# Out and down product with stationary weights, residual and result transposed, and squares of x moved up in a decoder block on one core

## The chip, the cores and the metric

One core of a Trainium2 chip runs the kernel. The metric is the device time in microseconds of one execution. A core has a matrix engine (TensorE, PE in the profile, with a row of its own, PEld, for loading the stationary operand), VectorE (DVE), ScalarE (ACT), GpSimd (POOL) and the queue engine SyncE (SP), which here issues the transfers of the weights. Each engine works through its own list in order; semaphores make one wait for another.

## The reference

A decoder block for 256 tokens of width 1024, all in float32:

```
n = rmsnorm(x, g1);  z = n @ w_in                       # 1024 x 7168, seven branches of 1024
y_conv = silu(layernorm(conv31(u * sigmoid(gate)))) @ w_conv_out
y_attn = attention(q, k, v with QK-norm and ALiBi, 8 heads) @ w_attn_out
merged = sigmoid(gc) * y_conv + sigmoid(ga) * y_attn
h   = x + merged @ w_out
out = h + (silu(m @ w_gate) * (m @ w_up)) @ w_down,     m = rmsnorm(h, g2)   # inner width 2816
```

Two parts matter here. The first RMS norm needs the sum of squares of each token of x over 1024 features; its factor is applied after the first products. The end of the block is the out product, the residual `h`, the second norm, gate and up product, and the down product with the residual added.

## The kernel before, in words

Every weight is float32 and is split into a high part (`whi`, a cast on ScalarE, line 154) and a low part (`wlo`, the difference, on VectorE or in some slots GpSimd, line 155); the activations are split in the same way. A product is three matmuls: high by high, low by high, high by low.

The work is a list of 146 slots, each with 512 KB of weights (128 partitions of 4 KB). The loop at the end of `hybrid_block` walks it. In each slot it first runs the closures in `pre`, then the first half of the slot's matmuls, issues the load and the split of weights for later slots (`AHEAD` = 6 slots for the split), runs `jobs`, then the second half, and then `post` and `late`. So the place of every instruction on every engine is set by the slot into which a closure was put. All engines follow the one written order.

There are two forms of a product. In `Chunk` slots the activations (transposed, features on partitions) are stationary and 512 columns of weights move; the result has tokens on partitions. `mm3` issues twelve matmuls of 512 columns a slot, six for each half of the tokens. In `Cols` slots a 128 x 128 tile of weights is stationary and the 256 tokens move; the result has output features on partitions. `mm_cols` issues 24 matmuls of 256 columns a slot. Before the change only gate-up (`gu`, 44 slots) is in the second form. In order, the slots are the convolution branch (16), q, k and v (24), the two gates (16), attention out (8), convolution out (`co`, 8), out product (`wo`, 8), `gu` (44) and down product (`dn`, 22).

The function `pair` makes the two tiles of a split activation; with `SHIFT` = 48 its data begin 48 floats, 192 bytes, into the tile. The pair `h`, which gate-up reads, has this shift; the pair `m`, which the out product reads, and the tiles `fh` and `fl`, which the down product reads, do not.

The start: x arrives transposed (`xt`); `split_x` makes its two parts, and `square` puts the squares of two k-tiles at a time on ScalarE, to be added on GpSimd (lines 713 and 715). `first_norm`, behind slot 4, sums them over the partitions with the matmul `ss` (line 727). VectorE and GpSimd make the factor `rstd` of it.

Around the out product: its result has tokens on partitions, is added to x in rows (`xs`, loaded for this, line 555), turned by sixteen transposes on PE (`htr`, line 565) and split from PSUM (`hh` on ScalarE, line 570, `hl` on VectorE, line 571). The sums of squares come from ScalarE's accumulator (line 577). The factor of the second norm is spread over the partitions by the product `rb` (line 607) as `row`; gate-up's gate half is multiplied by it, while its up half is not: that factor is applied with the residual when the down product is stored (`store`, line 651). The down product's last three slots are taken apart, so that the last store is small.

Of the kernel before, what the change touches and what calls it, by code (L numbers as in the profile page):

```python
# [82 lines left out]
GU_BANKS = ("cv0", "cv1", "mm", "mm", "mm", "mm")  # L83
GU_ORDER = halves_first(2 * KF, KD, len(GU_BANKS))


@with_exitstack
def hybrid_block(ctx: ExitStack, tc: tile.TileContext, x, xT, par, w_in, w_co, w_ao, w_o, w_gu, w_dn, out):
# [40 lines left out]
    def stream_dma(upto):  # L129
        while at["dma"] < min(upto, len(slots)):  # L130
            i = at["dma"]
            c, g = slots[i]
            raw[i] = wp.tile([P, *shape_of(i)], F32, tag="raw", bufs=RAW_BUFS, name=f"raw{i}")
            for part in parts(i):
                if i == 0:
                    load_x(part.start, part.stop)
                (nc.sync if i or part.start else nc.scalar).dma_start(raw[i][:, part, :], c.w[g][:, part, :])
                between(i, part)
            at["dma"] += 1
# [25 lines left out]
    def mm3(c, i, g, t, acc=None, cols=slice(0, CW), first=0, last=None):  # L165

        xh, xl = c.lhs()
        acc = c.acc[t] if acc is None else acc
        last = c.nk - 1 if last is None else last
        tok = slice(t * P, (t + 1) * P)  # L170
        for j in range(G):
            k = g * G + j
            nc.tensor.matmul(acc, xh[:, k, tok], hi[i][:, j, cols], start=(k == first), stop=False)  # L173
            nc.tensor.matmul(acc, xl[:, k, tok], hi[i][:, j, cols], start=False, stop=False)  # L174
            nc.tensor.matmul(acc, xh[:, k, tok], lo[i][:, j, cols], start=False, stop=(k == last))  # L175
# [3 lines left out]
    def mm_cols(c, i, g, units, slot):  # L179
        xh, xl = c.rhs()  # L180
        for u in units:
            n, k = c.order[g * U + u]
            c.seen[n] += 1
            first, last = c.seen[n] == 1, c.seen[n] == c.nk
            if first:
                tag = GU_BANKS[banks["n"] % len(GU_BANKS)]
# [11 lines left out]
    xt = ea.tile([P, XG + KD * S], F32, tag="vs", name="xt")  # L198
    xs = cst.tile([P, T, D], F32, name="xs")
# [318 lines left out]
    def merge_done(b):  # L518
        cols = slice(b * CW, (b + 1) * CW)

        def done(slot, acc):
# [6 lines left out]
            def turn():  # L528
                if not mT:
                    mT[0] = pair("m")  # L530
# [16 lines left out]
    s2 = sm.tile([P, 128], F32, bufs=1, name="s2")[:, : 2 * T].rearrange("p (t b) -> p t b", b=2)  # L547

    def out_done(b):
        cols = slice(b * CW, (b + 1) * CW)  # L550

        def done(slot, acc):
# [36 lines left out]
            late[slot + 2].append(squares)  # L589
        return done  # L590


    ff, gates, second = {}, {}, {}
# [5 lines left out]
    def spread2():  # L599
# [11 lines left out]
    def ffn_done(slot, n, acc):  # L611

# [25 lines left out]
        if not up:  # L638
            st["at"] = at_ = max(slot + 1, gu_slot + 5)
# [8 lines left out]
    def store(b, t, acc, cols=slice(0, CW)):  # L648
        to = slice(b * CW + cols.start, b * CW + cols.stop)
        o = sm.tile([P, cols.stop - cols.start], F32, tag="u", name=f"o{b}{t}{cols.start}")  # L650
        nc.vector.scalar_tensor_tensor(o, acc, rstd2[:, t : t + 1], xs[:, t, to], op0=ALU.mult, op1=ALU.add)
        nc.sync.dma_start(out[t * P : (t + 1) * P, to], o)

    def down_done(b):
        def done(slot, acc):
            if b == 0:
                late[slot + 1].append(lambda: [store(b, t, acc[t]) for t in range(T)])
        return done
# [17 lines left out]
    for b in range(2):  # L676
        add(Chunk(f"dn{b}", w_dn[b], lambda: ff[0], KF, down_done(b)))
# [39 lines left out]
    for i in range(6):  # L717
# [4 lines left out]
        if i >= 2:  # L722
            square(i - 2)
# [11 lines left out]
    late[16].append(lambda: nc.scalar.dma_start(xs, x.rearrange("(t p) d -> p t d", p=P)))  # L735
# [3 lines left out]
    n = len(slots)  # L739
    tail = 3  # L740
    split_k = KF - tail * G
    for slot, (c, g) in enumerate(slots):
# [7 lines left out]
        if rows and slot < n - tail:  # L750
            mm3(c, slot, g, 0)
# [6 lines left out]
        elif slot < n - tail:  # L758
            mm3(c, slot, g, 1, last=split_k - 1 if c is slots[-1][0] else None)
            if slot == n - tail - 1:  # L760
                end = xs[:, 1, D - CW :]
                nc.vector.scalar_tensor_tensor(end, c.acc[1], rstd2[:, 1:2], end, op0=ALU.mult, op1=ALU.add)
            for job in post.pop(slot, ()):
                job()
        elif slot == n - 1:
            for i in range(tail):
                mm3(c, n - tail + i, g - tail + 1 + i, 0)
            store(1, 0, c.acc[0])
            for part in range(2):
                cols = slice(part * CW // 2, (part + 1) * CW // 2)  # L770
                end = bank(f"end{part}", CW // 2)
                for i in range(tail):
                    mm3(c, n - tail + i, g - tail + 1 + i, 1, end, cols, first=split_k)
                store(1, 1, end, cols)
# [63 lines left out]
```

## Time and profile before

| | us |
|---|---|
| median of 3 timed runs | 440.75 (440.18 to 441.38) |
| the profiled execution, its own time | 441.83 |
| its span, first to last instruction | 440.0 |
| PE busy in the span | 433.4 (98%) |
| VectorE, ScalarE, GpSimd busy | 316.7, 247.8, 90.1 |

The busy share of PE is that of matmuls whose ends are modelled, and a matmul that waits for its operands can look busy. What PE does between two matmuls is read from their starts. The chain of waits gives 93% of the span to PE. The transfers move 182 GB/s on average and come several slots ahead of use after the first microseconds. The granted clock of TensorE is 1.00 nearly everywhere, with one dip in the first tenth of the span.

### The profile page before, as it was taken

How to read it: one execution, taken by the hardware profiler on the slowest of the kernel's cores; microseconds unless marked ns; L12 is line 12 of the kernel's file. 1: busy time of each engine (PE TensorE's matmuls, PEld its weight loads, DVE VectorE, ACT ScalarE, POOL GpSimd, SP SyncE). 2: the span in 40 equal slices, each digit the busy share in tenths (PEclk: the TensorE clock that was granted, in tenths of full speed). 3: DMA queues.
4: the chain of work that ended last, by engine and by line, in shares of the span. 5: the costliest groups of instructions: out<-in, count | busy, mean ns of one | idle time of the engine just before them, and what ended most of it. 6: DMA issues, size and time to landing. Idle time of an engine off the chain costs nothing.

```text
span 440.0 us, 6863 instructions
## 1 busy us (share of the span) xinstructions
PE 433.4 (98%) x2514; PEld 378.1 (86%) x2514; DVE 316.7 (72%) x558; ACT 247.8 (56%) x451; POOL 90.1 (20%) x74
## 2 busy tenths in 40 slices
PE   8899999999999999999999999999999999999996
PEld 4678888888888888888888899999999999888886
DVE  4989998998889799967759368666666666744501
ACT  6844466779998776558525267554444444533300
POOL 1615575643655424200000000000000000000000
PEclk9989999999999999999999999999999999999999
DMA  8975573556435435554745545555555555766101
GB/s 276 346 263 209 193 292 119 182 192 203 141 136 192 144 112 176 192 191 144 242 160 176 194 137 194 190 194 192 193 191 192 192 195 192 251 223 198 44 0 49
DMA packets 23346, 80.30 MB, mean 182 GB/s; under 512 B 2576, under 2 KB 3216, under 8 KB 23312
## 3 DMA queue, kind: packets, MB, share of 16 engines
q1 hardware_dynamic: 22752, 78.40, 52.7%
q10 hardware_dynamic: 560, 1.46, 0.9%
q8 instruction: 20, 0.33, 0.3%
q14 instruction: 14, 0.11, 0.1%
HBM read 78.80 MB, written 1.05 MB: 181 GB/s over the span
## 4 chain that ended last, share of the span: by engine, by line
PE 93%; ACT 2%; POOL 2%; DMA 1%; DVE 1%; SPq 0%; issue 0%
PE gu L191 9%; PE gu L192 9%; PE gu L190 9%; PE dn L174 4%; PE dn L175 4%; PE dn L173 4%; PE g L175 3%; PE g L173 3%; PE g L174 3%; PE conv L173 2%; PE conv L175 2%; PE conv L174 2%; PE k L175 2%; PE k L173 2%; PE v L175 2%; PE q L173 2%
## 5 line engine op out<-in xcount | busy, mean ns | idle before, releaser
L155 DVE TENSOR_TENSOR wlo<-raw,whi 128x1024 fp32r<-128x1024 f32 (+1 forms) x125 | 155.0, 1258 | 25.9 <-ACT whi L154 25.0
L154 ACT CAST whi<-raw 128x1024 fp32r<-128x1024 f32 (+1 forms) x149 | 150.4, 1033 | 36.7 <-PE dn L174 19.9
L190 PE MATMUL gu<-hh,whi 128*128 128x256 f32 x352 | 97.8, 278 | 0.0
L191 PE MATMUL gu<-hl,whi 128*128 128x256 f32 x352 | 97.6, 277 | 0.1
L192 PE MATMUL gu<-hh,wlo 128*128 128x256 f32 x352 | 97.4, 277 | 0.0
L273 DVE SCALAR_TENSOR_TENSOR cacc<-cv,prm,cacc 128x256 f32<-128x256 f32 x240 | 97.1, 474 | 0.2
L155 POOL TENSOR_TENSOR wlo<-raw,whi 128x1024 fp32r<-128x1024 f32 x24 | 60.7, 2536 | 50.4 <-ACT whi L154 45.5
L191 PEld LDWEIGHTS gu<-hl,whi 128*128 128x128 f32 x352 | 66.1, 188 | 0.4 <-DVE hl L571 0.3
L190 PEld LDWEIGHTS gu<-hh,whi 128*128 128x128 f32 x352 | 66.1, 188 | 0.3 <-ACT hh L570 0.2
L192 PEld LDWEIGHTS gu<-hh,wlo 128*128 128x128 f32 x352 | 66.2, 188 | 0.0
L175 PE MATMUL dn<-wlo,fh 128*128 128x512 f32 x82 | 31.9, 389 | 0.0
L174 PE MATMUL dn<-whi,fl 128*128 128x512 f32 x82 | 31.9, 389 | 0.0
L173 PE MATMUL dn<-whi,fh 128*128 128x512 f32 x82 | 31.9, 389 | 0.0
L173 PE MATMUL conv<-whi,xgh 128*128 128x512 f32 x64 | 26.3, 412 | 0.4 <-ACT whi L154 0.4
L173 PE MATMUL g<-whi,xgh 128*128 128x512 f32 x64 | 26.4, 412 | 0.0
L626 DVE TENSOR_TENSOR f<-gu,fs 128x256 f32<-128x256 f32 x22 | 9.2, 424 | 23.0 <-PE gu L192 23.0
L175 PE MATMUL conv<-wlo,xgh 128*128 128x512 f32 x64 | 25.7, 402 | 0.0
L174 PE MATMUL conv<-whi,xgl 128*128 128x512 f32 x64 | 25.7, 402 | 0.0
L175 PE MATMUL g<-wlo,xgh 128*128 128x512 f32 x64 | 25.1, 393 | 0.0
L174 PE MATMUL g<-whi,xgl 128*128 128x512 f32 x64 | 25.0, 390 | 0.0
L633 ACT CAST fh<-f 128x256 fp32r<-128x256 f32 x22 | 8.8, 406 | 26.8 <-DVE f L626 26.7
L622 ACT ACTIVATE fs<-fg 128x256 f32<-128x256 f32 x22 | 9.1, 417 | 25.4 <-DVE fg L618 25.4
(163 smaller groups left out, 747.6 us busy)
## 6 DMA issues: line engine op xcount, KB each, us to landing
raw<-in_w_in SPq DMA_DIRECT2D x53, 512.0 KB, 4.1
raw<-in_w_gu SPq DMA_DIRECT2D x44, 512.0 KB, 3.3
raw<-in_w_dn SPq DMA_DIRECT2D x22, 512.0 KB, 4.0
raw<-in_w_ao SPq DMA_DIRECT2D x8, 512.0 KB, 3.3
raw<-in_w_co SPq DMA_DIRECT2D x8, 512.0 KB, 3.3
raw<-in_w_o SPq DMA_DIRECT2D x8, 512.0 KB, 4.7
raw<-in_w_in SPq DMA_DIRECT2D x5, 256.0 KB, 5.6
xs<-in_x ACTq DMA_DIRECT2D x1, 1024.0 KB, 4.8
```

The costliest lines, as they stand in the source:

```text
L154: nc.scalar.copy(hi[i][:, part, :], r[:, part, :])
L155: eng.tensor_sub(lo[i][:, part, :], r[:, part, :], hi[i][:, part, :].bitcast(F32))
L173: nc.tensor.matmul(acc, xh[:, k, tok], hi[i][:, j, cols], start=(k == first), stop=False)
L174: nc.tensor.matmul(acc, xl[:, k, tok], hi[i][:, j, cols], start=False, stop=False)
L175: nc.tensor.matmul(acc, xh[:, k, tok], lo[i][:, j, cols], start=False, stop=(k == last))
L190: nc.tensor.matmul(acc, hi[i][:, u, :], xh[:, k, :], start=first, stop=False)
L191: nc.tensor.matmul(acc, hi[i][:, u, :], xl[:, k, :], start=False, stop=False)
L192: nc.tensor.matmul(acc, lo[i][:, u, :], xh[:, k, :], start=False, stop=last)
L273: nc.vector.scalar_tensor_tensor(cacc[j], src, w, cacc[j], op0=ALU.mult, op1=ALU.add)
L622: nc.scalar.activation(st["s"], st["g"], AF.Silu)
L626: nc.vector.tensor_mul(st["f"], acc, st["s"])
L633: nc.scalar.copy(ff[0][0][:, j, :], st["f"])
```

## The change

The out product and the down product become `Cols` slots, with weights stationary and 256 tokens moving. Their weights are laid out in 128 x 128 tiles on the host, in orders `O_ORDER` and `DN_ORDER` that take the first columns by halves of k. `xt` stays to the end; the residual is added to it in transposed form as each 128 output features are done, and the result is stored as 1024 x 256 and transposed on the host. The load of x in rows is gone, as are the transposes `htr`. The sum of squares for the second norm is now the squares of the transposed `h` (ScalarE), added up on GpSimd, and a small product `ss2` on PE. The up half of gate-up is multiplied by `row` as well. The pairs of `m` and `f` get the 192 bytes. At the start, the first two k-tiles of x are one transfer, all on SP's queue; the first two slots take their matmuls k-tile by k-tile for both halves of the tokens; and the squares of x stand one step earlier.

```diff
-GU_BANKS = ("cv0", "cv1", "mm", "mm", "mm", "mm")
-GU_ORDER = halves_first(2 * KF, KD, len(GU_BANKS))
+BANKS = ("cv0", "cv1", "mm", "mm", "mm", "mm")
+O_ORDER = halves_first(KD, KD, KD // 2)
+GU_ORDER = halves_first(2 * KF, KD, len(BANKS))
+DN_ORDER = halves_first(KD, KF, 2)
...
-                if i == 0:
-                    load_x(part.start, part.stop)
-                (nc.sync if i or part.start else nc.scalar).dma_start(raw[i][:, part, :], c.w[g][:, part, :])
+                if i == 0 and part.start == 0:
+                    load_x(0, 2)
+                nc.sync.dma_start(raw[i][:, part, :], c.w[g][:, part, :])
...
-    xt = ea.tile([P, XG + KD * S], F32, tag="vs", name="xt")
-    xs = cst.tile([P, T, D], F32, name="xs")
+    xt = cst.tile([P, XG + KD * S], F32, name="xt")
...
-                    mT[0] = pair("m")
+                    mT[0] = pair("m", SHIFT)
...
-            def evac():
-                for t in range(T):
-                    nc.vector.tensor_add(xs[:, t, cols], xs[:, t, cols], acc[t])
-
-            def turn():
-                if not hT:
-                    hT[0] = pair("h", SHIFT)
-                hh, hl = hT[0]
-                for k2 in (4 * b, 4 * b + 2):
-                    tr = bank(f"htr{k2}", 2, S)
-                    for j in range(2):
-                        for t in range(T):
-                            nc.tensor.transpose(tr[:, j, t * P : (t + 1) * P],
-                                                xs[:, t, (k2 + j) * P : (k2 + j + 1) * P], ident)
-                    for j in range(2):
-                        k = k2 + j
-                        g = prm[:, C_G2 + k : C_G2 + k + 1]
-                        nc.scalar.activation(hh[:, k, :], tr[:, j, :], AF.Copy, scale=g)
-                        nc.vector.scalar_tensor_tensor(hl[:, k, :], tr[:, j, :], g, hh[:, k, :].bitcast(F32),
-                                                       op0=ALU.mult, op1=ALU.subtract)
-
-            def squares():
-                for t in range(T):
-                    junk = sm.tile([P, CW], F32, tag="u", name="junk2")
-                    nc.scalar.activation(junk, xs[:, t, cols], AF.Square, accum_out=s2[:, t, b : b + 1])
-                if not b:
-                    second["ones"] = sm.tile([P, P], F32, tag="junk", bufs=1, name="allone")
-                    nc.gpsimd.memset(second["ones"], 1.0)
-                else:
-                    nc.vector.tensor_add(rstd2, s2[:, :, 0], s2[:, :, 1])
-                    rsqrt_mean(rstd2, rstd2, D, T)
-                    spread2()
-                    jobs[slot + 5].append(row2)
-
-            pre[slot + 1].append(evac)
-            jobs[slot + 2].append(turn)
-            late[slot + 2].append(squares)
...
+    def out_done(slot, j, acc):
+        h = xk(j, j + 1)[:, 0, :]
+        g = prm[:, C_G2 + j : C_G2 + j + 1]
+
+        def residual():
+            if not hT:
+                hT[0] = pair("h", SHIFT)
+            nc.vector.tensor_add(h, h, acc)
+
+        def high():
+            nc.scalar.activation(hT[0][0][:, j, :], h, AF.Copy, scale=g)
+
+        def low():
+            nc.vector.scalar_tensor_tensor(hT[0][1][:, j, :], h, g, hT[0][0][:, j, :].bitcast(F32),
+                                           op0=ALU.mult, op1=ALU.subtract)
+
+        def square2():
+            sq = free(f"hsq{j}")
+            nc.scalar.activation(sq, h, AF.Square)
+            if "sum" in second:
+                nc.gpsimd.tensor_add(second["sum"], second["sum"], sq)
+            else:
+                second["sum"] = free("hsum", "kT")
+                second["ones"] = sm.tile([P, P], F32, tag="junk", bufs=1, name="allone")
+                nc.gpsimd.memset(second["ones"], 1.0)
+                nc.gpsimd.tensor_copy(second["sum"], sq)
+
+        pre[slot + 1].append(residual)
+        late[slot + 1].append(high)
+        late[slot + 1].append(square2)
+        pre[slot + 2].append(low)
+        if j == KD - 1:
+            jobs[slot + 2].append(root2)
+            jobs[slot + 4].append(row2)
...
+    def root2():
+        ss = bank("ss2", T)
+        for t in range(T):
+            nc.tensor.matmul(ss[:, t : t + 1], second["sum"][:, t * P : (t + 1) * P], second["ones"][:, :1],
+                             start=True, stop=True)
+        nc.vector.tensor_scalar(rstd2, ss, 1.0 / D, EPS, op0=ALU.mult, op1=ALU.add)
+        nc.gpsimd.tensor_tensor(rstd2, rstd2, mhalf[:, :T], op=ALU.pow)
...
-            nc.vector.tensor_mul(st["f"], acc, st["s"])
+            nc.vector.tensor_mul(st["f"], acc, second["row"])
+            nc.vector.tensor_mul(st["f"], st["f"], st["s"])
...
-                ff[0] = (late_pool.tile([P, KF, S], F32R, name="fh"), late_pool.tile([P, KF, S], F32R, name="fl"))
+                ff[0] = tuple(
+                    late_pool.tile([P, KF * S + P], F32R, name="f" + x)[:, SHIFT : SHIFT + KF * S]
+                    .rearrange("p (k s) -> p k s", s=S) for x in "hl"
+                )
...
+    def down_done(slot, j, acc):
+        def evac():
+            o = sm.tile([P, S], F32, tag="u", name=f"o{j}")
+            nc.vector.tensor_add(o, acc, xk(j, j + 1)[:, 0, :])
+            nc.sync.dma_start(out[j * P : (j + 1) * P, :], o)
+
+        if j == KD - 1:
+            ends.append(evac)
+        else:
+            late[slot + 1].append(evac)
...
-    add(*(Chunk(f"wo{b}", w_o[b], lambda: mT[0], KD, out_done(b)) for b in range(2)))
+    add(Cols("wo", w_o, lambda: mT[0], KD, O_ORDER, out_done))
...
-        add(Chunk(f"dn{b}", w_dn[b], lambda: ff[0], KF, down_done(b)))
+    add(Cols("dn", w_dn, lambda: ff[0], KF, DN_ORDER, down_done))
...
-        if i >= 2:
-            square(i - 2)
+        if 1 <= i < 5:
+            square(i - 1)
...
-    late[16].append(lambda: nc.scalar.dma_start(xs, x.rearrange("(t p) d -> p t d", p=P)))
...
+        if slot < 2:
+            for j in range(G):
+                for t in range(T):
+                    mm3(c, slot, g, t, pieces=(j,))
+        elif rows:
```

On ScalarE at the start of the program, the casts of the weights (`whi`, the third to the sixth slot's) stand with the squares of x (`sq`, `xsq`) and its split (`xgh`). Before:

```order
L698 ACTIVATE xgh<-xt 128x256 x2
L154 CAST whi_170<-raw_134 128x512 x2
L698 ACTIVATE xgh<-xt 128x256 x2
L709 ACTIVATE sq_145<-xt 128x512
L154 CAST whi_181<-raw_138 128x1024
L712 ACTIVATE xsq_185<-xt 128x512
L154 CAST whi_188<-raw_140 128x1024
L712 ACTIVATE xsq_192<-xt 128x512
```

And after the change:

```order
L709 ACTIVATE sq_142<-xt 128x512
L156 CAST whi_168<-raw_131 128x512 x2
L698 ACTIVATE xgh<-xt 128x256 x2
L712 ACTIVATE xsq_178<-xt 128x512
L156 CAST whi_181<-raw_135 128x1024
L712 ACTIVATE xsq_185<-xt 128x512
L156 CAST whi_188<-raw_137 128x1024
L712 ACTIVATE xsq_192<-xt 128x512
L156 CAST whi_196<-raw_139 128x1024
```

All four squares stand ahead of the cast that they followed, the first of them ahead of the third slot's two casts.

On PE the out product (`wo`) is followed by gate-up (`gu`). Before, the transposes `htr` of the residual's second half stand among gate-up's matmuls in its second slot:

```order
L190 MATMUL gu_2621<-hh,whi_2495 128x256
L191 MATMUL gu_2621<-hl,whi_2495 128x256
L192 MATMUL gu_2621<-hh,wlo_2496 128x256
L565 MATMUL htr_2640<-ident,xs 128x128 x4
L565 MATMUL htr_2649<-ident,xs 128x128 x4
L190 MATMUL gu_2658<-hh,whi_2495 128x256
L191 MATMUL gu_2658<-hl,whi_2495 128x256
```

After the change `ss2`, the second sum of squares, stands in the same slot:

```order
L192 MATMUL gu_2740<-hl,whi_2565 128x256
L193 MATMUL gu_2740<-hh,wlo_2566 128x256
L597 MATMUL ss_2759<-allone,hsum 128x1 x2
L191 MATMUL gu_2767<-hh,whi_2565 128x256
L192 MATMUL gu_2767<-hl,whi_2565 128x256
L193 MATMUL gu_2767<-hh,wlo_2566 128x256
```

The eight transposes are gone here, as are the eight in the out product's last slot, and two short matmuls that read GpSimd's sum `hsum` have come in.

On VectorE in the out product, the low parts of the weights (`wlo`) stand with the residual. Before, the residual was two operations for each half of the columns, and `hl` came from the transposes:

```order
L155 TENSOR_TENSOR wlo_2514<-raw_2405,whi_2513 128x1024
L555 TENSOR_TENSOR xs<-xs,wo_0_2397 128x512
L555 TENSOR_TENSOR xs<-xs,wo_1_2398 128x512
L155 TENSOR_TENSOR wlo_2534<-raw_2423,whi_2533 128x1024
L155 TENSOR_TENSOR wlo_2552<-raw_2457,whi_2551 128x1024
L571 SCALAR_TENSOR_TENSOR hl<-htr_2557,prm,hh 128x256 x2
L571 SCALAR_TENSOR_TENSOR hl<-htr_2566,prm,hh 128x256 x2
L555 TENSOR_TENSOR xs<-xs,wo_0_2449 128x512
L555 TENSOR_TENSOR xs<-xs,wo_1_2450 128x512
```

After the change, each 128 features have an addition to `xt` and, a slot later, a low part `hl`:

```order
L559 TENSOR_TENSOR xt<-xt,wo_2393 128x256
L559 TENSOR_TENSOR xt<-xt,wo_2412 128x256
L157 TENSOR_TENSOR wlo_2520<-raw_2341,whi_2519 128x1024
L565 SCALAR_TENSOR_TENSOR hl<-xt,prm,hh 128x256 x2
L559 TENSOR_TENSOR xt<-xt,wo_2425 128x256
L559 TENSOR_TENSOR xt<-xt,wo_2458 128x256
L157 TENSOR_TENSOR wlo_2566<-raw_2359,whi_2565 128x1024
L565 SCALAR_TENSOR_TENSOR hl<-xt,prm,hh 128x256 x2
L559 TENSOR_TENSOR xt<-xt,wo_2550 128x256
L157 TENSOR_TENSOR wlo_2608<-raw_2406,whi_2607 128x1024
L565 SCALAR_TENSOR_TENSOR hl<-xt,prm,hh 128x256
```

The residual's operations are smaller and are spread over the out product's slots, one or two before each low part of the weights.

## Rows read from the trace of the kernel before

**Rows 1.** The page, busy time of PE and its share of the span.

```profile
PE 433.4 (98%) x2514; PEld 378.1 (86%) x2514; DVE 316.7 (72%) x558; ACT 247.8 (56%) x451; POOL 90.1 (20%) x74
```

**Rows 2.** Timeline of PE, 19.8 to 27.5: start, length, engine, line, operation, wait.

```profile
20.11 0.39 PE L175 MATMUL conv<-wlo,xgh 128*128 128x512 f32 x1
22.31 0.60 PE L727 MATMUL ss<-ones,sq 128*128 128x1 f32 x4 [1.80 <-POOL sq L715]
...
23.32 0.57 PE L175 MATMUL conv<-wlo,xgh 128*128 128x512 f32 x1
...
26.97 0.39 PE L175 MATMUL conv<-wlo,xgh 128*128 128x512 f32 x1
```

**Rows 3.** Busy time by stretch: PE, PEld, DVE, ACT, POOL, then granted clock, DMA.

```profile
23.40:26.70 3.30, 3.30 (x10) 2.53 (x9) 2.27 (x3) 0.21 (x1) 0.86 (x2) 0.50 0.86 290
...
254.20:256.30 2.10, 1.96 (x13) 1.52 (x12) 1.56 (x4) 1.52 (x5) 0.00 (x0) 1.00 0.21 86
...
269.80:370.00 100.20, 100.20 (x886) 100.20 (x885) 65.47 (x98) 52.07 (x79) 0.00 (x0) 1.00 0.59 200
```

**Rows 4.** Chain of waits: start, length, what.

```profile
259.39 0.87 PE htr L565 x8
```

**Rows 5.** Timeline of PE, gate-up up to the product rb.

```profile
254.65 0.38 PE L191 MATMUL gu<-hl,whi 128*128 128x256 f32 x1
...
256.28 0.28 PE L192 MATMUL gu<-hh,wlo 128*128 128x256 f32 x1
...
257.10 0.28 PE L190 MATMUL gu<-hh,whi 128*128 128x256 f32 x1
...
268.58 0.59 PE L607 MATMUL rb<-diag,allone 128*128 128x256 f32 x2
```

**Rows 6.** Timeline of PE, steady stretches of down product and gate-up.

```profile
409.81 0.39 PE L173 MATMUL dn<-whi,fh 128*128 128x512 f32 x1
...
411.17 0.39 PE L173 MATMUL dn<-whi,fh 128*128 128x512 f32 x1
...
289.78 0.28 PE L190 MATMUL gu<-hh,whi 128*128 128x256 f32 x1
...
290.46 0.28 PE L190 MATMUL gu<-hh,whi 128*128 128x256 f32 x1
```

**Rows 7.** Chain of waits, the last pieces of the down product.

```profile
435.05 0.12 PE end L174
```

**Rows 8.** Timeline of PE, ACT and DVE in the out product.

```profile
235.33 1.08 ACT L538 ACTIVATE mh<-mtr 128x512 fp32r<-128x512 f32 x2 [3.38 <-PE mtr L536]
...
235.49 0.48 PE L173 MATMUL wo<-whi,mh 128*128 128x512 f32 x1
...
235.96 0.69 DVE L539 SCALAR_TENSOR_TENSOR ml<-mtr,mh 128x512 fp32r<-128x512 f32 x1
```

**Rows 9.** Groups of instructions: shape, count, busy time, mean ns, idle before.

```profile
L618 DVE TENSOR_TENSOR fg<-gu,row 128x256 f32<-128x256 f32 x22 | 9.2, 423 | 15.2 <-PE gu L192 14.8 <-ACT row L609 0.4
```

**Rows 10.** Timeline of POOL at the start.

```profile
14.30 6.28 POOL L713 TENSOR_TENSOR sq<-sq,xsq 128x512 f32<-128x512 f32 x3 [11.81 <-ACT xsq L712]
20.66 1.59 POOL L715 TENSOR_TENSOR sq<-sq 128x256 f32<-128x256 f32 x1
```

**Rows 11.** Timeline of DVE at the start.

```profile
13.73 1.23 DVE L155 TENSOR_TENSOR wlo<-raw,whi 128x1024 fp32r<-128x1024 f32 x1 [0.72 <-ACT whi L154]
15.19 10.41 DVE L155 TENSOR_TENSOR wlo<-raw,whi 128x1024 fp32r<-128x1024 f32 x6 [0.24 <-ACT whi L154]
```

**Rows 12.** Timeline of ACT at the start.

```profile
12.13 0.62 ACT L709 ACTIVATE sq<-xt 128x512 f32<-128x512 f32 x1
12.66 1.04 ACT L154 CAST whi<-raw 128x1024 fp32r<-128x1024 f32 x1
13.60 0.63 ACT L712 ACTIVATE xsq<-xt 128x512 f32<-128x512 f32 x1
```

**Rows 13.** Timeline of PE, third matmul of slot 3.

```profile
15.35 0.39 PE L175 MATMUL conv<-wlo,xgh 128*128 128x512 f32 x1
```

More of the change, by code (lines that the diff above doesn't have):

```diff
@@ L80, in halves_first, with hybrid_block @@
     return out + [(c, k) for c in range(first, cols) for k in range(nk)]
-GU_BANKS = ("cv0", "cv1", "mm", "mm", "mm", "mm")
-GU_ORDER = halves_first(2 * KF, KD, len(GU_BANKS))
+BANKS = ("cv0", "cv1", "mm", "mm", "mm", "mm")
+O_ORDER = halves_first(KD, KD, KD // 2)
+GU_ORDER = halves_first(2 * KF, KD, len(BANKS))
+DN_ORDER = halves_first(KD, KF, 2)
 @with_exitstack
-def hybrid_block(ctx: ExitStack, tc: tile.TileContext, x, xT, par, w_in, w_co, w_ao, w_o, w_gu, w_dn, out):
+def hybrid_block(ctx: ExitStack, tc: tile.TileContext, xT, par, w_in, w_co, w_ao, w_o, w_gu, w_dn, out):
     nc = tc.nc
@@ L163, in pair, with mm3 @@
         )
-    def mm3(c, i, g, t, acc=None, cols=slice(0, CW), first=0, last=None):
+    def mm3(c, i, g, t, pieces=range(G)):
         xh, xl = c.lhs()
-        acc = c.acc[t] if acc is None else acc
-        last = c.nk - 1 if last is None else last
+        acc = c.acc[t]
         tok = slice(t * P, (t + 1) * P)
-        for j in range(G):
+        for j in pieces:
             k = g * G + j
-            nc.tensor.matmul(acc, xh[:, k, tok], hi[i][:, j, cols], start=(k == first), stop=False)
-            nc.tensor.matmul(acc, xl[:, k, tok], hi[i][:, j, cols], start=False, stop=False)
-            nc.tensor.matmul(acc, xh[:, k, tok], lo[i][:, j, cols], start=False, stop=(k == last))
+            nc.tensor.matmul(acc, xh[:, k, tok], hi[i][:, j, :], start=(k == 0), stop=False)
+            nc.tensor.matmul(acc, xl[:, k, tok], hi[i][:, j, :], start=False, stop=False)
+            nc.tensor.matmul(acc, xh[:, k, tok], lo[i][:, j, :], start=False, stop=(k == c.nk - 1))
     banks = {"n": 0}
@@ L185, in mm_cols @@
             if first:
-                tag = GU_BANKS[banks["n"] % len(GU_BANKS)]
+                tag = BANKS[banks["n"] % len(BANKS)]
                 banks["n"] += 1
@@ L197, in hybrid_block, with xk @@
     prm = cst.tile([P, N_PAR], F32, name="prm")
-    xt = ea.tile([P, XG + KD * S], F32, tag="vs", name="xt")
-    xs = cst.tile([P, T, D], F32, name="xs")
+    xt = cst.tile([P, XG + KD * S], F32, name="xt")
+    def xk(k0, k1):
+        return xt[:, XG + k0 * S : XG + k1 * S].rearrange("p (k s) -> p k s", s=S)
     warm = cst.tile([P, P], BF16, name="warm")
@@ L593, in hybrid_block @@
-    ff, gates, second = {}, {}, {}
+    second = {}
+    def out_done(slot, j, acc):
[27 more added lines that the diff above has]
+            jobs[slot + 4].append(row2)
@@ L595, in free @@
+    ff, gates = {}, {}
     def free(name, tag="qT"):
         return sm.tile([P, S], F32, tag=tag, bufs=4, name=name)
-    def spread2():
+    def root2():
[5 more added lines that the diff above has]
+        nc.gpsimd.tensor_tensor(rstd2, rstd2, mhalf[:, :T], op=ALU.pow)
@@ L638, in ffn_done @@
         if not up:
-            st["at"] = at_ = max(slot + 1, gu_slot + 5)
+            st["at"] = at_ = max(slot + 1, gu_slot + 4)
             pre[at_].append(scaled)
@@ L646, in ffn_done @@
             pre[at_ + 1].append(low)
[L648 to L658, printed above, removed]
+    ends = []
+    def down_done(slot, j, acc):
[7 more added lines that the diff above has]
+            late[slot + 1].append(evac)
     for p in range(KD // 2):
@@ L672, in hybrid_block @@
     add(*(Chunk(f"co{b}", w_co[b], lambda: yT[0], KD, merge_done(b)) for b in range(2)))
-    add(*(Chunk(f"wo{b}", w_o[b], lambda: mT[0], KD, out_done(b)) for b in range(2)))
+    add(Cols("wo", w_o, lambda: mT[0], KD, O_ORDER, out_done))
     gu_slot = len(slots)
     add(Cols("gu", w_gu, lambda: hT[0], KD, GU_ORDER, ffn_done))
-    for b in range(2):
-        add(Chunk(f"dn{b}", w_dn[b], lambda: ff[0], KF, down_done(b)))
+    add(Cols("dn", w_dn, lambda: ff[0], KF, DN_ORDER, down_done))
     xg[0] = pair("xg")
-    def xk(k0, k1):
-        return xt[:, XG + k0 * S : XG + k1 * S].rearrange("p (k s) -> p k s", s=S)
     def load_x(k0, k1):
@@ L734, in hybrid_block @@
     late[0].append(lambda: nc.scalar.dma_start(prm, par))
-    late[16].append(lambda: nc.scalar.dma_start(xs, x.rearrange("(t p) d -> p t d", p=P)))
     late[TABLE_SLOT].append(lambda: load_table(AF.Silu))
-    n = len(slots)
-    tail = 3
-    split_k = KF - tail * G
     for slot, (c, g) in enumerate(slots):
@@ L749, in hybrid_block @@
             c.acc = [ps.tile([P, CW], F32, tag="mm", bufs=4, name=f"{c.name}_{t}") for t in range(T)]
-        if rows and slot < n - tail:
+        if slot < 2:
[3 more added lines that the diff above has]
+        elif rows:
             mm3(c, slot, g, 0)
@@ L757, in hybrid_block @@
             mm_cols(c, slot, g, range(U // 2, U), slot)
[L758 to L774, printed above, removed]
+        elif slot >= 2:
+            mm3(c, slot, g, 1)
+        for job in post.pop(slot, ()):
+            job()
         load["pe"] += SLOT + pe_side.get(slot, 0.0)
@@ L781, in hybrid_block @@
             c.done(slot, c.acc)
+    for job in ends:
+        job()
     assert not (pre or jobs or post or late)
@@ L815 @@
     arrays = {
-        "x": x,
         "xT": np.concatenate([vec(i["norm1_g"]), np.zeros((P, XG - KD), np.float32),
@@ L822 @@
         "w_ao": cols(i["w_attn_out"][0]),
-        "w_o": cols(i["w_out"][0]),
+        "w_o": tiles(i["w_out"][0], O_ORDER),
         "w_gu": tiles(gu, GU_ORDER),
-        "w_dn": cols(i["w_ffn_down"][0]),
+        "w_dn": tiles(i["w_ffn_down"][0], DN_ORDER),
     }
@@ L832 @@
         args.append(nc.dram_tensor(f"in_{name}", a.shape, mybir.dt.from_np(a.dtype), kind="ExternalInput").ap())
-    o = nc.dram_tensor("out_0", (S, D), F32, kind="ExternalOutput").ap()
+    o = nc.dram_tensor("out_0", (D, S), F32, kind="ExternalOutput").ap()
     with tile.TileContext(nc) as tc:
@@ L836 @@
     r = run_bass_kernel_spmd(nc, [feed], core_ids=[0])
-    return r.results[0]["out_0"].reshape(1, S, D)
+    return np.ascontiguousarray(r.results[0]["out_0"].T).reshape(1, S, D)
```

5 lines of the change are left out of this document (removed).

## The prediction, on record before the changed kernel ran

> **What bounds the kernel now.** I read the page's busy table first: TensorE (PE) is busy 98% of the span [rows 1], so a change pays only where it shortens PE's own stream. I then took PE's timeline and looked for places where one matmul starts later after the last than its length asks. There are four, and nothing else on the chip matters.
>
> The start: PE's last matmul of slot 4 starts at 20.11, and the next instruction, the sum of squares `ss`, at 22.31 [rows 2]; less the 0.23 of the matmul itself that is a wait of 1.97 us, ended by POOL. Right behind it the granted clock is 0.50 [rows 3], that is 1.2 GHz: the nine matmuls from 23.32 to 26.97 take 3.65 us in place of 9 x 0.227 = 2.04, a loss of 1.6.
>
> The eight transposes `htr`, twice: the chain of waits gives 0.87 of its time to one such block [rows 4].
>
> The first gate-up slot: seven matmuls from 254.65 to 256.28 take 1.63 us [rows 5]; at the 0.118 of the matmuls behind them (256.28 to 257.10, seven in 0.82) they would take 0.82. They wait for the evictions of `htr`. Here the clock stays at 1.00 [rows 3], so gaps that add up to 0.8 us do not bring it down; 2 us did.
>
> The pace: a down matmul of 512 columns starts every 0.2267 us (six in 1.36), a gate-up matmul of 256 every 0.1133 (six in 0.68) [rows 6]. Before the small product `rb` at 268.58 [rows 5], though, gate-up runs at 0.118.
>
> **The change part by part.** Times are of the profiled execution, 441.83 us, of which the span is 440.0. The timed runs have their median at 440.75, 1.08 lower. I come back to that.
>
> *Out and down product with stationary weights.* 96 + 264 matmuls of 512 columns become 720 of 256. At the two paces that is 360 x 0.2267 = 81.6 us against 720 x 0.1133 = 81.6 [rows 6]: nothing. The form itself saves no PE time. Of the 264, the last 18 run today as 36 of 256 columns at 0.12 [rows 7]; in the steady stream they cost 36 x 0.0065 = **-0.2**. The end stays as it is: PE's last result, one VectorE operation, a store of 128 KB.
> The Trainium skill says otherwise of the form: "TensorE: Matmul & The Clock Gate", section "Back-to-back issue gap", gives 262 cycles for 256 columns and 518 for 512. Two halves would thus cost 6 cycles more than a whole, 2.5 ns at full clock, and 360 of them, by estimate, 0.9 us. The rows show two halves equal to a whole, so I do not take it; by the rule the forecast would be 0.9 higher.
>
> *Operands 192 bytes on.* The transposed operand of gate-up had the shift already, and its pace is the one above. The pairs for the out and down product get it too. I have no row of the unshifted form; the nearest is 0.118. Settling is not immediate: gate-up came to 0.1133 only seven matmuls after `rb`. I expect the out product to start the same way: 192 x 0.0045 = +0.85; gate-up until `rb`, now 3.5 slots instead of 5.5 (84 matmuls against 132), -0.2. Together **+0.6**; bounds 0 (settled at once) and +7.8 less today's 0.6 (all 1776 matmuls at 0.118).
>
> *Residual and result transposed.* Both `htr` blocks go: 2 x 0.87 = **-1.75**. The wait of the first gate-up slot goes if the new operands are in time: gate-up needs k-tiles 0 to 3 in its first three slots, and these belong to the out product's first four columns, done in its slots 2 and 3 (of 0 to 7), so the cover is four slots, 10.9 us. Columns 4 to 7 are asked for from gate-up slot 3; the last is split in its slot 1. I take **-0.8**, bounds 0 and -0.8.
> The out product needs k-tiles 4 to 7 of the merged operand at its slot 2, two slots sooner. Today `mh` starts at 235.33, `ml` at 235.96, and PE resumes at 235.49 [rows 8]; six matmuls of 512 take it to 236.9. `ml`'s first half ends at 236.65, its second 0.6 later at 237.25 and is wanted six matmuls of 256 into the slot, at 237.6. In time by some 0.3: 0, with up to +1 if VectorE is late.
>
> *The new second sum.* `ss2` on PE: like `ss`, four passes of 0.60 [rows 2], of which the next matmul covers a little: **+0.55**. It stands in the middle of gate-up slot 1, 4.1 us (1.5 slots of 2.72) behind the out product's last matmul, and waits for the last addition on POOL. That chain: drain and VectorE queue with the residual, 0.8 (an operation of 0.42 [rows 9]); two ScalarE operations, 0.95 (I put each a little above that 0.42); one POOL addition of 128x256, 1.59 [rows 10]. Sum 3.4, cover 0.7. If additions take the 2.1 of the larger ones (6.28 for three [rows 10]) the cover is 0.2; if VectorE lags by an operation of 1.7 (10.41 for six beside POOL's additions [rows 11]), PE waits about 1. I take 0, bounds 0 and +2. Queued behind it on PE is all of gate-up.
> The extra product by the row is 22 x 0.42 = 9.3 us on VectorE [rows 9], which over 100.2 us of gate-up is busy 65.5 [rows 3]: hidden. Were VectorE full, all 9.3 would show. The load of x in rows, 1 MB, was waited for by nobody.
>
> *The start.* On ScalarE the first square that POOL uses moves ahead of one weight cast: 13.60 becomes 12.66 [rows 12]. POOL's chain, 14.30 to 22.25 [rows 10], begins 0.94 earlier and ends at 21.31. Against it, the cast of slot 3 moves behind a square, 0.53 (12.13 to 12.66 [rows 12]), so that slot's low part, 13.73 to 14.96 [rows 11], ends at 15.49. PE wants it with the slot's third matmul, 15.35 today [rows 13]. Taking the first two slots piece by piece lets PE do both token tiles on what has landed; I estimate 0.3 (a group of three less behind the last piece is 0.68, and slot 1 waits most of it away on its own low part). So PE comes at 15.05, waits 0.44, reaches `ss` at 20.48 and waits 0.83 there. `ss` starts at 21.31 instead of 22.31: **-1.0**, bounds 0 and -2.0. A wait of 0.8 is the size that left the clock alone at 255 us, so I count the slow stretch as gone: **-1.6**, bounds 0 and -1.6. Later slots keep their splits slots ahead, so this lead carries to the end.
>
> Sum: +0.6 - 0.2 - 1.75 - 0.8 + 0.55 - 1.0 - 1.6 = **-4.2**, or 437.6 on the profiled execution's time and 436.55 on the median. The timed runs may each have met less of the clock's drop than the profiled one, which would also be why they are faster; then less is to be had from them. I take **437.0**.
>
> **Rivals.**
> *A, the forecast:* own range 435.2 to 438.2.
> *B, the start does not pay.* PE still meets a wait long enough for the clock to fall, because POOL's chain of 8 us is only moved. For it: the chain stays four additions in a row. Against: the wait halves. Price 1.6, giving 438.6.
> *C, the second sum comes late* by 1 to 2 us, through VectorE and POOL in the out product: for it the cover of 0.2 to 0.7; against it, VectorE has room in each slot (0.42 + 0.48 + at most 1.73 of 2.72). About 438.5.
> *D, the slow pace holds in the out and down product* (place of the operands): 528 down matmuls x 0.0045 = +2.4, giving 439.4.
> *E, the slow pace holds in all three,* from the out product's first matmul to the end, because what ended it at `rb` was not `rb`. For it: neither `htr` nor the waits ended it. Against: from seven matmuls after `rb` to the end of gate-up no matmul is slow. 972 + 528 more matmuls x 0.0045 = +6.8: 443.8, slower. It decides from about 540 further slow matmuls: the gain is then below 0.3%.
>
> **How the numbers follow.** A 0.62, B 0.14, C 0.09, D 0.08, E 0.07. Less than 0.3% (1.3 us) cannot be told from no change here. A, B and C are faster, 0.85; D lies at the border and is counted as the same, 0.08; E is slower, 0.07. The range 435.0 to 439.6 takes in A to D.
>
> **What the profile after would show.** `ss` at 21.3 or earlier and PEclk 1.00 behind it (B: 0.50 again); a short wait before the third matmul of slot 3; out product and down product at 0.1133 a start (D, E: 0.118); no gap at the first gate-up matmuls; `ss2` without a wait for POOL (C: with one). Wrong would be a PE wait in the out product's slot 2, or any stretch where the lead won at the start is lost again before 230 us.

## The result, and the profile after

The changed kernel takes **443.55 us** (median of 4 runs, 443.49 to 443.61), against 441.06 (440.18 to 441.48) for the kernel before on the same chip: ratio 1.0069, 95% interval 1.0049 to 1.0089. It is slower, outside the range of the forecast, and within 0.3 us of rival E (443.8). The profiled execution took 443.61, its span 441.8.

The page's busy table of the changed kernel answers to [rows 1], the granted clock in its 40 slices to the dip of [rows 3]:

```profile
PE 436.5 (99%) x2844; PEld 395.3 (89%) x2844; DVE 326.1 (74%) x586; ACT 248.2 (56%) x451; POOL 91.9 (21%) x81
...
PEclk9999999999999999999999999999999999999999
```

The clock no longer drops, and PE is busy 99% of a longer span: the time went into PE's own stream. Next PE's timeline at the start, beside [rows 2, 13] (start, length, engine, line, operation, wait):

```profile
14.72 0.39 PE L175 MATMUL conv<-whi,xgl 128*128 128x512 f32 x1
15.68 0.50 PE L176 MATMUL conv<-wlo,xgh 128*128 128x512 f32 x1 [0.58 <-DVE wlo L157]
...
20.58 0.39 PE L176 MATMUL conv<-wlo,xgh 128*128 128x512 f32 x1
20.80 0.57 PE L727 MATMUL ss<-ones,sq 128*128 128x1 f32 x4
...
227.52 0.28 PE L191 MATMUL wo<-mh,whi 128*128 128x256 f32 x1
```

The third matmul of slot 3 starts 0.96 after the second: a wait of 0.74. `ss` follows the matmul before it by 0.22: no wait at all, 1.51 us earlier than before, and no half clock behind it. The out product starts at 227.52; before it was 230.61. The start gave 3.1 us. The first and the last addition of the squares on GpSimd (POOL), beside [rows 10], and the out product's start in the kernel before:

```profile
13.21 1.34 POOL L713 TENSOR_TENSOR sq<-sq,xsq 128x512 f32<-128x512 f32 x1 [10.70 <-ACT xsq L712]
...
19.11 1.61 POOL L715 TENSOR_TENSOR sq<-sq 128x256 f32<-128x256 f32 x1
```

```profile
230.61 0.39 PE L173 MATMUL wo<-whi,mh 128*128 128x512 f32 x1
```

POOL's chain ends at 20.72, just ahead of `ss`.

Busy time by stretch in the three products (PE, PEld, DVE, ACT, POOL, granted clock, DMA), beside [rows 3, 6]:

```profile
234.00:246.00 12.00, 12.00 (x104) 12.00 (x104) 10.87 (x16) 8.15 (x15) 3.77 (x5) 1.00 0.56 185
270.00:370.00 100.00, 100.00 (x851) 100.00 (x850) 68.46 (x107) 47.97 (x71) 0.00 (x0) 1.00 0.55 185
380.00:430.00 50.00, 50.00 (x427) 50.00 (x426) 20.35 (x22) 14.33 (x14) 0.00 (x0) 1.00 0.44 141
```

This is where the time went. A count takes in the one to three matmuls that reach over a stretch's edges; 100 us hold 851 matmuls of gate-up, where before 100.2 held 886 [rows 3]. Matmul by matmul they start at 118, 117, 118 ns, mean **117.8**, in all three products to the very end. VectorE and ScalarE have room in all three stretches, and the clock is at 1.00, so neither operands nor the clock set this.

PE's timeline around the two small products of gate-up, `ss2` (shown as `ss`) and `rb`, beside [rows 5]:

```profile
255.13 0.28 PE L193 MATMUL gu<-hh,wlo 128*128 128x256 f32 x1
255.25 0.50 PE L597 MATMUL ss<-allone,hsum 128*128 128x1 f32 x4
255.61 0.36 PE L191 MATMUL gu<-hh,whi 128*128 128x256 f32 x1
255.81 0.28 PE L192 MATMUL gu<-hl,whi 128*128 128x256 f32 x1
...
261.35 0.60 PE L607 MATMUL rb<-diag,allone 128*128 128x256 f32 x2
261.60 0.47 PE L191 MATMUL gu<-hh,whi 128*128 128x256 f32 x1
261.90 0.28 PE L192 MATMUL gu<-hl,whi 128*128 128x256 f32 x1
262.02 0.28 PE L193 MATMUL gu<-hh,wlo 128*128 128x256 f32 x1
```

`ss2` waits for nobody and costs some 0.45 (0.36, and a first matmul behind it that takes 0.20 for 0.12). Behind `rb` the starts stay 0.118 apart, where before they went to 0.1133 within seven matmuls. No `htr` stands in the chain of waits any more, and there is no gap at the start of gate-up.

### The profile page after: what moved, and what is told of

The parts are those of the page before. It is cut to its first block, busy times and chain, and to the rows that moved or that the text cites. A ratio compares the mean times of both kernels' runs of the same rounds, so it can differ in the third digit from the quotient of the medians.

```text
span 441.8 us, 7576 instructions
## 1 busy us (share of the span) xinstructions
PE 436.5 (99%) x2844; PEld 395.3 (89%) x2844; DVE 326.1 (74%) x586; ACT 248.2 (56%) x451; POOL 91.9 (21%) x81
## 4 chain that ended last, share of the span: by engine, by line
PE 96%; DMA 1%; ACT 1%; SPq 1%; DVE 0%; issue 0%
PE gu L191 9%; PE gu L193 9%; PE gu L192 9%; PE dn L191 5%; PE dn L193 5%; PE dn L192 5%; PE g L176 3%; PE g L174 3%; PE g L175 3%; PE conv L176 3%; PE conv L174 3%; PE conv L175 3%; PE wo L193 2%; PE wo L191 2%; PE wo L192 2%; PE k L176 2%
## 5 line engine op out<-in xcount | busy, mean ns | idle before, releaser
L157 DVE TENSOR_TENSOR wlo<-raw,whi 128x1024 fp32r<-128x1024 f32 (+1 forms) x125 | 153.3, 1240 | 19.3 <-ACT whi L156 18.3
L157 POOL TENSOR_TENSOR wlo<-raw,whi 128x1024 fp32r<-128x1024 f32 x24 | 58.2, 2429 | 51.4 <-ACT whi L156 46.5
L191 PE MATMUL dn<-fh,whi 128*128 128x256 f32 x176 | 49.5, 281 | 0.0
L192 PE MATMUL dn<-fl,whi 128*128 128x256 f32 x176 | 49.5, 281 | 0.0
L193 PE MATMUL dn<-fh,wlo 128*128 128x256 f32 x176 | 49.5, 281 | 0.0
L193 PEld LDWEIGHTS dn<-fh,wlo 128*128 128x128 f32 x176 | 33.8, 192 | 0.0
L192 PEld LDWEIGHTS dn<-fl,whi 128*128 128x128 f32 x176 | 33.0, 188 | 0.0
L191 PEld LDWEIGHTS dn<-fh,whi 128*128 128x128 f32 x176 | 33.0, 188 | 0.0
L625 DVE TENSOR_TENSOR f<-gu,row 128x256 f32<-128x256 f32 x22 | 9.3, 423 | 23.8 <-PE gu L193 23.8
L656 DVE TENSOR_TENSOR o<-dn,xt 128x256 f32<-128x256 f32 x8 | 3.4, 425 | 30.1 <-PE dn L193 30.1
```

Source lines behind the costliest of these rows:

```text
L157: eng.tensor_sub(lo[i][:, part, :], r[:, part, :], hi[i][:, part, :].bitcast(F32))
L625: nc.vector.tensor_mul(st["f"], acc, second["row"])
L656: nc.vector.tensor_add(o, acc, xk(j, j + 1)[:, 0, :])
```

## The experiments

Question: what decides whether matmuls of 256 columns start every 117.8 or every 113.3 ns? First, whether the new **places in memory** do (the tile of x moved, and with it every later tile by 64 bytes), or the **offset** of the operand, or something in the **order of the work**. Four kernels.

**Places as before, in the changed kernel** (192 bytes more make 256 with the 64, so that places counted in steps of 256 bytes are the old ones).

```
     prm = cst.tile([P, N_PAR], F32, name="prm")
+    cst.tile([P, 48], F32, name="pad")
     xt = cst.tile([P, XG + KD * S], F32, name="xt")
```

> The changed kernel with an unused tile of 192 bytes ahead of all others, so that every tile lies 256 bytes further than in the kernel before, counted in 256-byte steps at the same place. The distances between weights and operands stay as they are. Theory place (the slow pace of 0.118 us comes from the 64 bytes by which the larger xt has moved everything): gate-up falls to 0.1133 after rb and the down product stays there, 1500 matmuls x 0.0045 = 6.7 us less, 436.9 us. Theory phase (which of two paces PE falls into hangs on what happens around rb, not on places): 443.5 us, all matmuls of 256 at 0.118.

Measured: 443.31 (443.2 to 443.92), ratio 1.0067 (1.0042 to 1.0092). 117.8 ns throughout.

**Places as after, in the kernel before.**

```
     prm = cst.tile([P, N_PAR], F32, name="prm")
+    cst.tile([P, 16], F32, name="pad")
```

> The kernel before with an unused tile of 64 bytes ahead of all others: every tile lies where the changed kernel has it, nothing else is different. Theory place: gate-up stays at 0.118 after rb, 924 matmuls x 0.0045 = 4.2 us more, 445.2 us. Theory phase: 441.0 us, 0.1133 from seven matmuls after rb.

Measured: 440.16 (439.72 to 441.78), ratio 0.999 (0.9971 to 1.0009). Gate-up is fast, and from within its first slot on, behind a wait of 0.52. The 64 bytes are not the cause.

**No offset, in the changed kernel.**

```
-SHIFT = 48
+SHIFT = 0
```

> The changed kernel with SHIFT = 0, operands at the weights' place in steps of 256 bytes. It prices the shift in the stationary-weights form. If the shift does what gate-up's fast pace in the kernel before suggests, a matmul of 256 takes 0.118 or more; a pace of 0.120 (as in the last pieces of the down product before) would add 1776 x 0.002 = 4 us to 443.5. If the shift has no part in it: 443.5 us, 0.118.

Measured: 447.44 (447.24 to 447.64), ratio 1.0161 (1.0115 to 1.0207). Its 100 us of gate-up hold 836 matmuls, 120.0 ns:

```profile
270.00:370.00 100.00, 100.00 (x836) 100.00 (x835) 67.20 (x106) 46.77 (x70) 0.00 (x0) 1.00 0.53 180
```

So the offset does act in the changed kernel, in all three products; it brings 117.8 instead of 120.0, and not 113.3.

**The new start alone, in the kernel before** (order of loads, of squares, first two slots piece by piece; the diff is those hunks of the change).

```
-        if i >= 2:
-            square(i - 2)
+        if 1 <= i < 5:
+            square(i - 1)
...
+        if slot < 2:
+            for j in range(G):
+                for t in range(T):
+                    mm3(c, slot, g, t, pieces=(j,))
```

> The kernel before with the part of the change at the start alone (two k-tiles of x in one transfer, first weights on SP's queue, two slots taken k-tile by k-tile, squares one step earlier). By the prediction's terms: 1.0 less wait at ss and 1.6 less half clock, 441.1 - 2.6 = 438.5 us; ss at 21.3, PEclk 1.00 behind it; gate-up as before, 0.1133 after rb. If the timed runs of before meet the half clock less often than the profiled one: 439.5 to 440.

Measured: 438.28 (437.67 to 439.7), ratio 0.995 (0.9928 to 0.9972): the start is worth its 3 us. And its gate-up shows what I was looking for. PE's timeline of the variant in the first gate-up slot:

```profile
252.64 0.38 PE L190 MATMUL gu<-hh,whi 128*128 128x256 f32 x1
253.16 0.39 PE L191 MATMUL gu<-hl,whi 128*128 128x256 f32 x1
253.38 0.28 PE L192 MATMUL gu<-hh,wlo 128*128 128x256 f32 x1
253.50 0.28 PE L190 MATMUL gu<-hh,whi 128*128 128x256 f32 x1
253.62 0.28 PE L191 MATMUL gu<-hl,whi 128*128 128x256 f32 x1
253.73 0.28 PE L192 MATMUL gu<-hh,wlo 128*128 128x256 f32 x1
253.84 0.28 PE L190 MATMUL gu<-hh,whi 128*128 128x256 f32 x1
253.96 0.28 PE L191 MATMUL gu<-hl,whi 128*128 128x256 f32 x1
```

Ahead of the wait (0.52 between 252.64 and 253.16) the pace was 118; four matmuls behind it, it is 113, and stays. In the kernel before, a wait of the same size at the same place was followed by 118 (256.28 to 257.10 in [rows 5]):

```profile
255.53 0.38 PE L190 MATMUL gu<-hh,whi 128*128 128x256 f32 x1
256.05 0.39 PE L191 MATMUL gu<-hl,whi 128*128 128x256 f32 x1
```

Thus two theories. **W**: a wait that empties PE ends the slow pace, and the changed kernel has none. **R**: any interruption of the stream draws one of two paces anew, which an undisturbed stream then keeps.

**Fifteen interruptions with a wait**, every fifth slot from the out product's second (work added, nothing left out):

```
+    kt = cst.tile([P, 64], F32, name="kt")
...
+    def kick():
+        a = bank("kicka", T)
+        nc.tensor.matmul(a[:, :1], ident, ones, start=True, stop=True)
+        nc.scalar.copy(kt[:, :1], a[:, :1])
+        b = bank("kickb", T)
+        nc.tensor.matmul(b[:, :1], ident, kt[:, :1], start=True, stop=True)
...
+    for s in range(gu_slot - 7, len(slots), 5):
+        jobs[s].append(kick)
```

> The changed kernel with 15 interruptions of TensorE, one every fifth slot from the second slot of the out product on, each of which makes it wait: a one-column fp32 product with the identity, a copy of it by ScalarE, and a product that needs the copy. Each should cost 0.8 to 1.3 us of TensorE (its eight passes and a wait of 0.3 to 0.8 us), 12 to 20 us in all on 443.5. Theory W (a wait of TensorE with nothing left to run ends the slow pace, as the waits of 0.28 and 0.52 us did at the start of the gate-up product in the two variants of the kernel before): the product runs at 113.3 ns from the first or second interruption to the end, so nearly all of 1776 matmuls gain 4.5 ns, 8 us: about 451. Theory R (any interruption only draws the pace anew): stretches of 113.3 and of 117.8 ns between interruptions, or the fast one from some later interruption on; 452 to 459. Theory N (the pace is set by something else in the changed kernel): 117.8 everywhere, 456 to 463.

Measured: 455.84 (455.82 to 455.85), ratio 1.0327 (1.023 to 1.0424). Stretches between interruptions:

```profile
249.20:255.20 6.00, 6.00 (x56) 6.00 (x55) 5.11 (x7) 4.28 (x8) 1.74 (x3) 1.00 0.53 174
257.00:261.20 4.20, 4.20 (x37) 4.20 (x37) 2.87 (x5) 0.00 (x0) 0.72 (x1) 1.00 0.55 155
...
354.20:366.80 12.60, 12.60 (x110) 12.60 (x109) 7.76 (x12) 6.08 (x9) 0.00 (x0) 1.00 0.53 173
369.80:381.20 11.40, 11.40 (x103) 11.40 (x103) 7.50 (x12) 5.28 (x9) 0.00 (x0) 1.00 0.54 186
384.00:396.00 12.00, 12.00 (x104) 12.00 (x104) 7.00 (x8) 4.67 (x6) 0.00 (x0) 1.00 0.72 251
```

56 matmuls in 6.0 us, then 37 in 4.2; 110 in 12.6, then 103 in 11.4, then 104 in 12.0: with the one to three over the edges, and start by start in the trace, fast, slow, slow, fast, slow. Of the 15 waits two were followed by the fast pace, and both times the next interruption ended it (the first time `ss2`). W falls; an interruption can bring either pace, and end either.

**The same places without a wait**: two one-column products that need nothing.

```
+    def kick():
+        for x in "ab":
+            a = bank("kick" + x, T)
+            nc.tensor.matmul(a[:, :1], ident, ones, start=True, stop=True)
...
+    for s in range(gu_slot - 7, len(slots), 5):
+        jobs[s].append(kick)
```

> The same 15 places, but without a wait: two one-column fp32 products with the identity, that need nothing. Each should cost some 0.5 to 0.6 us (eight passes of 0.03 to 0.11, and a first product behind them that starts 0.2 late), 8 us in all. Theory W: no wait, so 117.8 ns everywhere, as behind the second sum and the row factor of the changed kernel: about 451. Theory R: some stretches at 113.3, 444 to 450. Theory N: 117.8 everywhere, 451, so that this run alone does not tell W from N.

Measured: 443.53 (443.24 to 448.42), ratio 1.0086 (1.0049 to 1.0124): with 15 interruptions it is as fast as the changed kernel without any.

```profile
233.00:246.00 13.00, 13.00 (x113) 13.00 (x112) 11.69 (x17) 9.32 (x17) 3.76 (x5) 1.00 0.58 190
248.30:255.30 7.00, 7.00 (x64) 7.00 (x63) 6.04 (x8) 4.93 (x8) 1.48 (x2) 1.00 0.58 193
256.20:261.00 4.80, 4.80 (x43) 4.80 (x42) 2.80 (x5) 0.00 (x0) 0.72 (x1) 1.00 0.59 188
263.40:275.80 12.40, 12.40 (x111) 12.40 (x111) 9.87 (x19) 7.13 (x12) 0.00 (x0) 1.00 0.46 151
...
404.20:416.00 11.80, 11.80 (x107) 11.80 (x106) 4.87 (x6) 4.61 (x5) 0.00 (x0) 1.00 0.18 59
```

Slow behind the first (which has `mtr` right behind it), fast behind the second, slow again from `ss2`, fast behind the third (with `rb` behind it) and behind each of the other twelve, into the down product. So no wait is needed, and the down product with stationary weights can run at 113.3.

**Other offsets**, 64 and 128 bytes (`SHIFT = 16`, `SHIFT = 32`).

> The changed kernel with the operands 64 bytes past the weights' place instead of 192. If the steady pace goes by the offset alone, the three products run at one pace from start to end, between 113.3 and 120.0 ns: 436 (113.3), 443.5 (117.8) or 447.4 (120.0, as with no offset). If the offset only allows the fast pace and history chooses it, as with 192: 443.5 again.

> The same with 128 bytes. By the same reading 436, 443.5 or 447.4; an offset that gives 113.3 from the first matmul of the out product on would show that the slow pace is not one of the changed order of work, but of this offset.

Measured: 443.51 (443.25 to 444.04), ratio 1.0073 (1.0056 to 1.0091), at 117.8 throughout; and 445.82 (445.74 to 445.9), ratio 1.01 (1.0005 to 1.0195), at 120.0 up to `rb` and at 118.7 behind it. Neither offset gives 113.3 by itself.

**One interruption only**, behind `rb`, without a wait and with one:

```
+    jobs[gu_slot + 4].append(kick)
```

> The changed kernel with one interruption only: two one-column fp32 products with the identity, eight passes without a wait, in the middle of the fifth slot of the gate-up product, behind the row factor, at about 265 us. Theory R (an interruption draws the pace anew and an undisturbed run of the product keeps it; eight such passes drew the fast one in the run with 15 of them): 113.3 ns from there to the end of the down product, some 1464 matmuls x 4.5 ns = 6.6, less 0.5 for the passes: 437.4. If the fast pace needs interruptions again and again, or had to do with the row factor just behind the passes: 117.8 to the end, 444.0.

> The same place, with the interruption that makes TensorE wait for a copy of ScalarE. Theory R: the length of the wait is chance, so is the pace: by the 15 of the run before (2 fast) most likely 117.8 to the end, 443.5 + 1.0 = 444.5, and in single runs 438. If any interruption at this place, behind the row factor, brings the fast pace: 438.

Without a wait: **437.41** (437.05 to 438.29), ratio **0.9922** (0.9901 to 0.9942), the version that beats both kernels. With a wait: 438.21 (437.7 to 442.48), ratio 0.9955 (0.993 to 0.9981); ten of its twelve runs lie at 437.7 to 438.5, and two at 442.4, these with a mean granted clock of 0.995 where the ten have 0.999 or more. The two left no trace, and at the slow pace I had expected 444.5, so what made them longer is open. PE's timeline of the former at the interruption, and its stretches:

```profile
264.19 0.28 PE L193 MATMUL gu<-hh,wlo 128*128 128x256 f32 x1
264.31 0.28 PE L614 MATMUL kicka<-ones,ident 128*128 128x1 f32 x2
264.45 0.36 PE L614 MATMUL kickb<-ones,ident 128*128 128x1 f32 x2
264.67 0.37 PE L191 MATMUL gu<-hh,whi 128*128 128x256 f32 x1
264.87 0.28 PE L192 MATMUL gu<-hl,whi 128*128 128x256 f32 x1
265.00 0.28 PE L193 MATMUL gu<-hh,wlo 128*128 128x256 f32 x1
265.11 0.28 PE L191 MATMUL gu<-hh,whi 128*128 128x256 f32 x1
```

```profile
270.00:370.00 100.00, 100.00 (x885) 100.00 (x884) 70.81 (x111) 49.45 (x73) 0.00 (x0) 1.00 0.57 190
380.00:430.00 50.00, 50.00 (x443) 50.00 (x442) 17.32 (x20) 12.65 (x12) 0.00 (x0) 1.00 0.36 119
```

885 matmuls in the 100 us that held 851, 443 in the 50 that held 427, and nothing else was changed: 6.1 us between the medians (6.0 to the next variant, run beside it), for an addition of 0.45 (four passes in the trace, where I had expected eight). The pace is the whole of what the changed kernel lost. For the version with a wait I had expected the slow pace, since only 2 of 15 waits had brought the fast one; that was wrong at this place, in the trace and, by their times, in ten runs of twelve.

**The row factor one slot later**, nothing added:

```
-            jobs[slot + 4].append(row2)
+            jobs[slot + 5].append(row2)
...
-            st["at"] = at_ = max(slot + 1, gu_slot + 4)
+            st["at"] = at_ = max(slot + 1, gu_slot + 5)
```

> The changed kernel with the row factor (and the first gate products, that need it) one slot of the gate-up product later, nothing added: as in the kernel before, where the factor stood five slots behind. Theory R: a new draw at about 264.5, at no cost: 436.9 if fast (1470 matmuls x 4.5 ns less), 443.5 if slow, with nothing to say beforehand which; the runs should agree among themselves, since no wait of chance length stands ahead of it. If the place of the row factor decides nothing: 443.5.

Measured: 443.44 (443.25 to 443.96), ratio 1.0059 (1.0039 to 1.0079), 851 matmuls in the same 100 us. `rb`, at this place too, keeps the slow pace; an interruption of another kind at nearly the same time does not.

## Why the prediction was wrong

The step that failed is the pace, "settling is not immediate: gate-up came to 0.1133 only seven matmuls after `rb`. I expect the out product to start the same way", sized at +0.6. I took 0.118 for a phase that passes and `rb` for what ends it. It is a pace of its own that lasts: 1776 matmuls x 4.5 ns = 8.0, less the 0.6 that the kernel before had of it, **+7.4**, the pace that rival E foresaw. The forecast's own upper bound for the term, 7.8 less 0.6, was nearly of that size (1776 x 0.0045 is 8.0, not 7.8), but the range stopped at D. The one switch in the trace of before was one outcome of an interruption. The same trace had the counter-evidence, as the rival said: `htr` and two waits had interrupted the slow stream and not ended it. One of four is no rule, and 0.07 was too little for E.

The other terms, in the profiled executions:

- *The form itself*, -0.2 for the tail: not resolved. At the fast pace two halves equal a whole (885 matmuls in 100 us); at the slow one they are 2 x 117.8 = 235.6 against 226.7 [rows 6]. The Trainium skill, "TensorE: Matmul & The Clock Gate", section "Back-to-back issue gap", gives one gap for each size, and calls it that of isolated matmuls; by it, as an estimate, the pair would cost 2.5 ns more. The runs show 0 or 9.
- *Transposes* -1.75 and *first gate-up slot* -0.8: as forecast, both gone. No wait in the out product's slot 2.
- *Second sum* +0.55: 0.45, without a wait; rival C did not happen.
- *Start* -1.0 and *half clock* -1.6: -1.5 and -1.6. The wait for slot 3 was 0.74 rather than 0.44, but POOL's chain ended at 20.72 and not at 21.31, having begun a little earlier and taken 7.5 rather than 8.0, so `ss` had no wait left. Rival B did not happen. That the timed runs of the kernel before met the drop of the clock only in part, as the forecast supposed, shows in the 17 runs beside the last variants: seven with a mean clock of 0.999 or more took 439.6 to 440.3, ten at 0.995 or 0.996 took 441.25 to 441.9 (in the variant with 64 bytes the two do not go together so plainly).

Together: 7.4 - 0.2 - 1.75 - 0.8 + 0.45 - 1.5 - 1.6 = +2.0; the profiled executions differ by 443.61 - 441.83 = 1.8. With the pace mended for all but the first 300 matmuls (192 of the out product, 4.5 slots of gate-up) the kernel stands at 437.4, near the 437.0 of the forecast.

Still open: what in an interruption chooses the pace. Its kind does not (`rb` ended the slow pace before and kept it after; the four passes of `ss2` ended the fast pace, four like them with other operands kept it twelve times), nor does a wait. But it does not look like chance either. In the seven traces with the 192 bytes `ss2` was always followed by the slow pace; the two products without a wait, where nothing else stands behind them, by the fast one 14 times of 14; the waits by the slow pace all nine times where PE waited 0.30 for ScalarE, and by the fast one three times of seven where it waited 0.25. So when the stream resumes, to within hundredths of a microsecond, may decide; it was not tested. For one program the choice mostly repeats: by their times all four runs of the changed kernel and all six of the one with the later row factor had the slow pace, all six of the best version the fast one.

## What to carry to other kernels

A pace of one instruction kind that appears at two levels in one trace is not "settling": count in how many of the places where it could have changed it did, before pricing a change that multiplies such instructions. Where a long undisturbed stream of equal matmuls runs some per cent slow with a full clock and its operands in time, insert one cheap foreign product and look at the pace behind it; measure this for each program, since which interruption helps could not be told beforehand.

## What I had not expected

Matmuls of 256 columns with 128x128 weights ran at lasting paces that went with the operand's place: 120.0 ns with operand and weights at the same place, 117.8 or 113.3 with the operand 192 bytes on; 4.5 ns is 3.8% of a product. With the 192 bytes the trace also shows the slow pace on the weight loads: of the three of a group, one is longer. The groups of weight loads of the changed kernel, then of the best version (line, operation, names, shape, count, busy us, mean ns):

```profile
L193 PEld LDWEIGHTS gu<-hh,wlo 128*128 128x128 f32 x352 | 67.5, 192 | 0.0
L192 PEld LDWEIGHTS gu<-hl,whi 128*128 128x128 f32 x352 | 66.2, 188 | 0.0
L191 PEld LDWEIGHTS gu<-hh,whi 128*128 128x128 f32 x352 | 66.1, 188 | 0.0
```

```profile
L192 PEld LDWEIGHTS gu<-hl,whi 128*128 128x128 f32 x352 | 66.2, 188 | 0.0
L193 PEld LDWEIGHTS gu<-hh,wlo 128*128 128x128 f32 x352 | 66.1, 188 | 0.0
L191 PEld LDWEIGHTS gu<-hh,whi 128*128 128x128 f32 x352 | 66.1, 188 | 0.0
```

192 against 188 for one of three, and 188 for all where the pace is fast. With no offset, at 120.0, all three take 192; with 64 bytes, though, all three take 187 to 188 at 117.8, so the longer load is not in every case the sign of the slower pace. That the load of the next weights and the read of the operand disturb each other, in a relation that a steady stream keeps, would fit the first two and the effect of the offset; it was not tested.
